# Ple product in the up projection's PSUM tiles, one norm chain for two pairs, weight tile and Gelu table loaded earlier

## The chip, the cores and the metric

The kernel runs on one core of a Trainium2 chip. The core has five engines, each with its own in-order stream of instructions: TensorE (PE, matmul), VectorE (DVE), ScalarE (ACT), GpSimd (POOL) and SyncE (SP, which mostly issues DMAs). Work passes between them through semaphores. The metric is the device time of one execution in microseconds, as the median of three runs. Every time below is in microseconds from the start of the profiled span, unless it says otherwise.

## The reference, cut to what matters

One layer of an encoder is applied to 1024 prompt frames and 32 sample frames, which the kernel handles together as 1056 columns.

```python
h = rms_norm(x, g_pre_mix)
z = h @ w_in                      # attention, HGRN2 and gate parts
ya = sink_attention(...)          # sliding window
yb = rms_norm(hgrn2(...)) * silu(ob)
mix = sigmoid(ga) * (ya @ w_br_a) + sigmoid(gb) * (yb @ w_br_b)
x = x + rms_norm(mix @ w_out, g_post_mix)          # output projection, x1
hf = rms_norm(x, g_pre_ffn)
a, u = split(hf @ w_up, 2)                         # up projection, 2 x 2816 columns
a = conv3(a)                                       # causal, depthwise
ffn = (gelu(a) * u) @ w_down
x = x + rms_norm(ffn, g_post_ffn)
x = x + (pe @ w_ple) * sigmoid(x @ w_ple_gate)     # "ple product" is pe @ w_ple
```

D_MODEL is 1024, D_FF 2816, and the width of pe 256. All is float32.

## The kernel before, in words

A float32 product is made of three matmuls in the form that TensorE reads quickly: both operands are split into a rounded part and a remainder, and high by high, low by high and high by low are added up in PSUM. These are the lines L200, L201 and L202 for an ordinary product (function `product`, through `block`, which takes a PSUM tile of one bank named `mm`) and L1835, L1836 and L1837 in the up projection (PSUM tiles named `st`).

The layer runs as a sequence of stages. The frames lie in four groups g of 264 columns (H = 264), which makes two pairs p, and the model dimension in eight tiles c of 128 rows. The stages around the change are:

- **Output projection.** For each pair p the loop runs over the eight row tiles c. Each step takes one weight tile of `w_out`, which was loaded by DMA as `wr` and split by ScalarE and VectorE into `wh` and `wl` (L181, L184), makes the two products of the pair and passes each to `z_out`, where ScalarE evicts it with a gain into `z` (L1449), squares it into `sq` (L1454), and VectorE adds the squares up (L1455). `next_w(n)` hands out a weight tile and keeps n tiles ahead loaded. During pair 1 the rest of the work of pair 0 is done beside it: `pair_norm(0, 0.25 / D)` turns sums of squares into the factors of the norm, `x1_part` adds the old x, `x1_squares` makes the squares of the new x, and a second call `pair_norm(0, 1.0 / D)` makes the factors of the next norm.
- **pair_norm.** TensorE multiplies the squares by a column of ones (`sums88`, L1475) into a PSUM bank named `tr`. VectorE works out the reciprocal roots in twelve small instructions on 128x6 elements. TensorE then transposes them (L301), and ScalarE copies the rows to `rbT` (L303).
- **Operand parts.** The up projection goes by a scheme with seven products of half-size blocks (Strassen's form), so its operands are sums and differences of blocks. `build_ops` makes them for the first pair of groups, and `op_part` for the second: ScalarE rounds (L1546), VectorE takes the remainder (L1547).
- **Ple product.** `ple_product(g)` makes, for each of the four groups, eight products of 128x264, in `mm` tiles; ScalarE copies each to `ple` (L1590), and a DMA on GpSimd's queue stores four at a time to `ple_d` (L1592). The table `beside`, filled through `at(m, f)`, names the work that is put behind the m-th of the 32 products: the adding of x for pair 1 (`x1_sum`, L1502, L1503), its gains (`x1_gain`, L1509), and the operand parts of the second pair.
- **Up projection.** Units of seven weight tiles each. Tiles 0 to 6 of unit 0 were split ahead, put to DRAM (`pw_d`), and come back by `load_part`; from unit 1 on, `unit_parts` makes them from raw weights `wu`: four sums of blocks (L1621, L1622, L1623, L1628, with the engine chosen as `adder`), a cast on ScalarE (L1614) and a remainder on VectorE (L1615). The results in PSUM are combined through `Sp` and `us` (L1846 to L1864). `ff_tail` is the end of a row tile: bias and first tap on ScalarE, two taps on VectorE (L1792), Gelu on ScalarE (L1794), gates on VectorE (L1795 to L1797).
- Unit 0 is special. It runs as two halves, one for each pair, and `last_ops` puts beside it what is left of the norm of pair 1.

The order within each engine comes from a scheduler that works from the code's order and from priorities (`behind(E)` puts a piece behind the work of an engine), and each engine then keeps this order: an instruction that waits holds back all that stand behind it on its engine. Pages of SBUF (`page(lq, i, ...)`) and buffers of pools are reused, and a transfer into one waits until its last reader has finished.

Of the kernel before, what the change touches and what calls it, by code (L numbers as in the profile page):

```python
# [59 lines left out]
def layer_kernel(  # L60
# [146 lines left out]
    def rsqrt(pool, out, v, n):  # L207

        bits = pool.tile([P, n], I32, tag="rsb", name=nm("rsb"), bufs=2)
        t = pool.tile([P, n], F32, tag="rst", name=nm("rst"), bufs=2)  # L210
# [1266 lines left out]
    def pair_norm(p, scale, t=None, late=False):  # L1477
# [3 lines left out]
        v = fo.tile([P, 6], F32, tag="nv", name=nm("nv"), bufs=2)  # L1481
        rs = fo.tile([P, 6], F32, tag="nr", name=nm("nr"), bufs=2)
# [4 lines left out]
        rsqrt(fo, rs[:], v[:], 6)  # L1487
# [18 lines left out]
    def x1_gain(g, i, ks=range(4)):  # L1506

        for k in ks:
            S.mul(z[g][:, 4 * i + k, :].bitcast(F32), x1q[g][i][:, k, :], g_ffn[:, 4 * i + k:4 * i + k + 1])  # L1509
# [24 lines left out]
    def x1_add(g):  # L1534

        a, b = x1q[g]
        V.tensor_tensor(a, a, b, op=ALU.add)
        V.tensor_tensor(a[:, 0:2, :], a[:, 0:2, :], a[:, 2:4, :], op=ALU.add)
# [43 lines left out]
    def ple_product(g, beside):  # L1582
        xs = pT.pop(g)
        for c in range(8):
            if c % 4 == 0:
                t = oz.tile([P, 4, H], F32, tag="x4", name=nm("ple"), bufs=3)
            b = block(ple_w[c // 4], slice((c % 4) * P, (c % 4 + 1) * P),
                      [xs[:, 0, k, :] for k in range(2)], [xs[:, 1, k, :] for k in range(2)],
                      ((0, 0), (1, 1)), H)
            S.copy(t[:, c % 4, :], b[:, :H])  # L1590
# [16 lines left out]
    def unit_parts(u, s1, place, out):  # L1607
# [10 lines left out]
        adder = V if u < 2 else G  # L1618
# [75 lines left out]
    for p in range(2):  # L1694
        for c in range(8):
            if p and c == 5:
                load_ple()
            w = next_w(2)
# [16 lines left out]
            if 2 <= c < 6:  # L1715
# [17 lines left out]

    for i in range(4):
        load_part(i)
    rows = pair_norm(1, 0.25 / D, late=True)
# [15 lines left out]
    at(6, rows, on=(E,))  # L1752
# [20 lines left out]
    qctx.close()  # L1773
    qctx = ExitStack()
    pf = qctx.enter_context(tc.tile_pool(name="pf", bufs=1, space=PSUM, reuse_waits="tile"))
# [24 lines left out]
    def last_ops(n):  # L1800
# [6 lines left out]
        with behind(S, V):  # L1807
# [306 lines left out]
```

## Time and profile before

| what | us |
| --- | --- |
| median of 3 runs | 2009.11 |
| the three runs | 2009.81, 2007.66, 2009.11 |
| the profiled execution | 2006.23 |
| its span | 2004.2 |
| pair 1 of the output projection | 1104 to 1158 |
| ple product | 1158 to 1185.3 |
| up projection, unit 0 | 1187.1 to 1211.5 |
| up projection, unit 1 | 1211.5 to 1233 |

The profiled execution is 2.03 us longer than its span, and 2.88 us shorter than the median. The stages follow from the lines that TensorE runs: L200 to L202 with `Ra`, `Rb` and `wh` in the output projection, with `pc` and `wq` in the ple product, and L1835 to L1837 in the up projection. A row such as "1150.34 0.63 PE L1475 ... [1.65 <-DVE sq L1528]" gives a start, a duration, the engine, the line, the operation and its tiles; the bracket says how long the engine had been idle and which instruction let it go on. A matmul of 264 columns is listed at 0.28 us, but the next one starts 0.12 us after it, since they overlap.

### The profile page before, as it was taken

What the parts mean: (1) busy time and instruction counts of PE and PEld (TensorE: products, weight loads), DVE (VectorE), ACT (ScalarE), POOL (GpSimd) and SP (SyncE); (2) the same over time, 40 slices, a digit from 0 to 9 for tenths busy, and PEclk for the clock granted to TensorE, in tenths of its full rate; (3) what the DMA queues carried; (4) which work ended last, traced back from release to release, by engine and by line L of the source; (5) the groups of instructions that cost most, each with busy time, mean ns of one, the idle gap of its engine ahead of it and who ended that gap; (6) DMA issues with size and microseconds to landing.
All of it is one profiled execution on the core that took longest, in us unless ns stands there. A gap on an engine that the chain in (4) does not pass through costs nothing. (4 is left out here: it accounts for less than half of the span.)

```text
span 2004.2 us, 37385 instructions
## 1 busy us (share of the span) xinstructions
PE 1981.8 (99%) x14304; PEld 1952.1 (97%) x14304; DVE 1423.3 (71%) x3150; ACT 967.7 (48%) x2178; POOL 224.8 (11%) x319
## 2 busy tenths in 40 slices
PE   8999999999999999999999999999999999999998
PEld 7899999999999999999999999999999999999998
DVE  6788888688888888553455778888878784655552
ACT  7555566556666666442224663333333344444432
POOL 1110100000000000002001123333333210000000
PEclk9999999999999999999999999999999999999999
DMA  7622311411111111477558582222222245655542
GB/s 257 154 92 85 107 52 55 152 43 58 58 39 53 37 54 54 136 235 220 164 173 278 182 278 66 84 75 86 76 86 76 86 140 195 212 191 173 170 130 80
DMA packets 253639, 247.47 MB, mean 123 GB/s; under 512 B 13893, under 2 KB 221912, under 8 KB 253461
## 3 DMA queue, kind: packets, MB, share of 16 engines
q1 hardware_dynamic: 245141, 218.59, 35.1%
q0 software_dynamic: 8240, 26.44, 3.8%
q8 instruction: 112, 1.84, 0.4%
q14 instruction: 66, 0.54, 0.1%
q10 hardware_dynamic: 80, 0.07, 0.0%
HBM read 177.56 MB, written 65.32 MB: 121 GB/s over the span
## 5 line engine op out<-in xcount | busy, mean ns | idle before, releaser
L1835 PE MATMUL st<-op,wt 128*128 128x264 f32 x1232 | 348.3, 283 | 3.5 <-ACT ple L1590 1.7
L1837 PE MATMUL st<-op,wt 128*128 128x264 f32 x1232 | 349.5, 284 | 0.0
L1836 PE MATMUL st<-op,wt 128*128 128x264 f32 x1232 | 347.7, 282 | 0.0
L184 DVE TENSOR_TENSOR wl<-wr,wh 128x1024 fp32r<-128x1024 f32 x129 | 157.9, 1224 | 118.9 <-ACT wh L181 105.5
L1835 PEld LDWEIGHTS st<-op,wt 128*128 128x128 f32 x1232 | 231.1, 188 | 4.6 <-ACT ple L1590 1.9
L1836 PEld LDWEIGHTS st<-op,wt 128*128 128x128 f32 x1232 | 231.4, 188 | 0.0
L1837 PEld LDWEIGHTS st<-op,wt 128*128 128x128 f32 x1232 | 230.8, 187 | 0.0
L181 ACT CAST wh<-wr 128x1024 fp32r<-128x1024 f32 x116 | 121.8, 1051 | 197.1 <-PE mm L201 149.7
L200 PE MATMUL mm<-La,wh 128*128 128x384 f32 (+1 forms) x528 | 174.4, 331 | 0.1
L200 PE MATMUL mm<-ac,wh 128*128 128x352 f32 x528 | 170.8, 324 | 1.3 <-DVE Sp L1864 1.3
L201 PE MATMUL mm<-Lb,wh 128*128 128x384 f32 (+1 forms) x528 | 170.9, 324 | 0.5 <-DVE Lb L710 0.4
L202 PE MATMUL mm<-La,wl 128*128 128x384 f32 (+1 forms) x528 | 170.5, 323 | 0.2 <-DVE wl L685 0.2
L201 PE MATMUL mm<-ac,wh 128*128 128x352 f32 x528 | 169.1, 320 | 0.0
L202 PE MATMUL mm<-ac,wl 128*128 128x352 f32 x528 | 169.1, 320 | 0.0
L1614 ACT CAST wt<-wu 128x512 fp32r<-128x512 f32 x126 | 77.7, 619 | 188.5 <-POOL ab L1821 93.8
L200 PE MATMUL mm<-Ra,wh 128*128 128x264 f32 x512 | 145.5, 284 | 0.0
L201 PE MATMUL mm<-Rb,wh 128*128 128x264 f32 x512 | 145.0, 283 | 0.0
L202 PE MATMUL mm<-Ra,wl 128*128 128x264 f32 x512 | 145.0, 283 | 0.0
L1615 DVE TENSOR_TENSOR wt<-wu,wt 128x512 fp32r<-128x512 f32 x126 | 101.0, 804 | 39.7 <-ACT wt L1614 39.7
L462 ACT ACTIVATE sc<-sc,st 128x257 f32<-128x257 f32 (+1 forms) x144 | 69.7, 485 | 73.2 <-DVE st L457 72.6
L201 PEld LDWEIGHTS mm<-Lb,wh 128*128 128x128 f32 x528 | 99.4, 188 | 1.7 <-DVE Lb L710 1.4
L200 PEld LDWEIGHTS mm<-ac,wh 128*128 128x128 f32 x528 | 99.0, 188 | 1.6 <-DVE Sp L1864 1.6
(496 smaller groups left out, 5692.8 us busy)
## 6 DMA issues: line engine op xcount, KB each, us to landing
wr<-in_w_down_dram SPq DMA_DIRECT2D x66, 512.0 KB
wu<-in_w_up_dram SPq DMA_DIRECT2D x42, 512.0 KB
wu<-in_w_in_dram SPq DMA_DIRECT2D x32, 512.0 KB
wr<-in_w_in_dram SPq DMA_DIRECT2D x25, 512.0 KB
ac<-act_d SPq DMA_DIRECT2D x66, 176.0 KB
act_d<-Up SPq DMA_DIRECT2D x21, 528.0 KB
wr<-in_w_out_dram SPq DMA_DIRECT2D x16, 512.0 KB
pw_d<-pw POOLq DMA_DIRECT2D x11, 512.0 KB, 5.3
```

The costliest lines, as they stand in the source:

```text
L181: S.copy(hi[:], raw[:])
L184: V.tensor_tensor(lo[:], raw[:], hi[:].bitcast(F32), op=ALU.subtract)
L200: E.matmul(ps, wh, a, start=first and n == 0, stop=False)
L201: E.matmul(ps, wh, b, start=False, stop=False)
L202: E.matmul(ps, wl, a, start=False, stop=last and n == len(ks) - 1)
L462: S.activation(sc[:m_, h, b0:e_ + 1], sc[:m_, h, b0:e_ + 1], AF.Exp, bias=st[:m_, 0, h:h + 1], scale=-1.0, accum_out=st[:m_, 1, h:h + 1])
L1614: S.copy(t[:, 0], src)
L1615: V.tensor_tensor(t[:, 1], src, t[:, 0].bitcast(F32), op=ALU.subtract)
L1835: E.matmul(o, wh, xh, start=first and k == 0, stop=False, skip_group_check=True)
L1836: E.matmul(o, wh, xl, start=False, stop=False, skip_group_check=True)
L1837: E.matmul(o, wl, xh, start=False, stop=k == 3, skip_group_check=True)
```

## The change

The ple product takes its PSUM from the pool `pf` of the up projection, which is now opened ahead of it. Two row tiles go to the two banks of one `st` tile, and one ScalarE copy of 128x528 takes the place of two of 128x264. The second norm of pair 0 and the first norm of pair 1 become one chain: their sums of squares go to one `tr` bank, one series of small VectorE instructions on twelve columns makes all factors, and `rows(1)` and `rows(0)` put the transposes behind the sixth and ninth ple products. Two of the operand parts of the first pair are written in the ple product's table, and the load of x for group 3 is put behind product 3 (page 0 instead of 1). One of four gains of groups 2 and 3 goes to VectorE. The last `w_out` tile is prepared one step earlier. The four sums of blocks of unit 1's weights go to GpSimd, as those of all later units did. In `last_ops`, `x1_add` is cut in two and spread over one more step, and a Gelu of one column is put there, whose result is overwritten later.

Line numbers after the change differ (L1601 is the copy that was L1590, L1865 to L1867 are the matmuls L1835 to L1837, L1632 is L1621).

```diff
@@ x_load, pair_norm, x1_gain, x1_add @@
-            t = page(lq, g - 2, [P, 8, H], "x")[:].bitcast(F32)
+            t = page(lq, 3 - g, [P, 8, H], "x")[:].bitcast(F32)
...
-            S.mul(z[g][:, 4 * i + k, :].bitcast(F32), x1q[g][i][:, k, :], g_ffn[:, 4 * i + k:4 * i + k + 1])
+            o, x, gain = z[g][:, 4 * i + k, :].bitcast(F32), x1q[g][i][:, k, :], g_ffn[:, 4 * i + k:4 * i + k + 1]
+            if g > 1 and k == 3:
+                V.tensor_scalar(o, x, gain, None, op0=ALU.mult)
+            else:
+                S.mul(o, x, gain)
...
         a, b = x1q[g]
         V.tensor_tensor(a, a, b, op=ALU.add)
+
+    def x1_fold(g):
+
+        a, b = x1q[g]
@@ ple_product @@
-            b = block(ple_w[c // 4], slice((c % 4) * P, (c % 4 + 1) * P),
-                      [xs[:, 0, k, :] for k in range(2)], [xs[:, 1, k, :] for k in range(2)],
-                      ((0, 0), (1, 1)), H)
-            S.copy(t[:, c % 4, :], b[:, :H])
+            if c % 2 == 0:
+                b = pf.tile([P, 2, 512], F32, tag="st", name=nm("st"), bufs=3)
+            product(b[:, c % 2, :H], ple_w[c // 4], slice((c % 4) * P, (c % 4 + 1) * P),
+                    [xs[:, 0, k, :] for k in range(2)], [xs[:, 1, k, :] for k in range(2)],
+                    ((0, 0), (1, 1)))
+            if c % 2:
+                S.copy(t[:, c % 4 - 1:c % 4 + 1, :], b[:, :, :H])
@@ unit_parts @@
-        adder = V if u < 2 else G
+        adder = V if u < 1 else G
@@ output projection @@
-            w = next_w(2)
+            w = next_w(2 + (p and c > 3))
...
-            if 2 <= c < 6:
+            if 2 <= c < 5:
                 next(op0)
...
             if c == 6:
-                for _ in op0:
-                    pass
                 x_load(2)
-                x_load(3)
-                with behind(E):
-                    rows = pair_norm(0, 1.0 / D, late=True)
                 p_load(2)
                 p_load(3)
-            if c == 7:
-                with behind(E):
-                    rows()
-
+
+    qctx.close()
+    qctx = ExitStack()
+    pf = qctx.enter_context(tc.tile_pool(name="pf", bufs=1, space=PSUM, reuse_waits="tile"))
     for i in range(4):
         load_part(i)
-    rows = pair_norm(1, 0.25 / D, late=True)
+    t = tr_bank()
+    v = fo.tile([P, 12], F32, tag="nv", name="nv2", bufs=1)
+    rs = fo.tile([P, 12], F32, tag="nr", name="nr2", bufs=1)
+    V.memset(v[:], 1.0)
+    for g in (0, 1):
+        sums88(t[:, 6:12], g, [sqz[g]])
+    for g in (2, 3):
+        sums88(t, g, [sqz[g]])
+    for a, sc in ((0, 0.25 / D), (6, 1.0 / D)):
+        V.tensor_scalar(v[:88, a:a + 6], t[:88, a:a + 6], sc, EPS, op0=ALU.mult, op1=ALU.add)
+    rsqrt(fo, rs[:], v[:], 12, 1)
+
+    def rows(p):
+        for h in range(2):
+            o, a = H * (2 * p + h), 6 * (1 - p) + 3 * h
+            norm_rows(rs[:, a:a + 3], T88, rbT[:, o:o + H])
...
-    at(6, rows, on=(E,))
+    for m in (0, 2):
+        at(m, next, op0)
+    at(3, x_load, 3)
+    at(6, rows, 1, on=(E,))
+    at(9, rows, 0, on=(E,))
@@ last_ops @@
-            elif n < 4:
-                x1_add(n)
-            elif n < 6:
-                op_part(1, n, (b11, b21)[n - 4])
+            elif n == 2:
+                x1_add(2)
+            elif n == 3:
+                x1_fold(2)
+                x1_add(3)
+                S.activation(us0[:, 0:1], ones[:], AF.Gelu_apprx_tanh)
+            else:
+                if n == 4:
+                    x1_fold(3)
+                if n < 6:
+                    op_part(1, n, (b11, b21)[n - 4])
```

The order on the engines shows three places. The first is TensorE at the start of unit 0, whose first half works through seven weight tiles, twelve matmuls each. `wt_14982` (before) and `wt_14933` (after) name the same tile, the fifth one, which comes from `pw_d` into a page that weights of the ple product (`wq`) held. Before, it is used behind the twelve matmuls each of four tiles, 48 in all, of which these rows show the end:

```order
L1837 MATMUL st_14961<-op_14336,wt_14595 128x264
L1835 MATMUL st_14962<-op_14423,wt_14982 128x264 [waits DMAHW0_49]
L1836 MATMUL st_14962<-op_14423,wt_14982 128x264
L1837 MATMUL st_14962<-op_14423,wt_14982 128x264
L1835 MATMUL st_14962<-op_14423,wt_14982 128x264
L1836 MATMUL st_14962<-op_14423,wt_14982 128x264
```

After the change, with 24 matmuls ahead of it:

```order
L1867 MATMUL st_14912<-op_14265,wt_14552 128x264
L1865 MATMUL st_14912<-op_14265,wt_14552 128x264
L1866 MATMUL st_14912<-op_14265,wt_14552 128x264
L1867 MATMUL st_14912<-op_14265,wt_14552 128x264
L1865 MATMUL st_14913<-op_14597,wt_14933 128x264 [waits DMAHW0_49,Activation_49]
L1865 MATMUL st_14911<-op_14338,wt_14554 128x264 [waits DMAHW5_49,Activation_49]
L1866 MATMUL st_14911<-op_14338,wt_14554 128x264
L1867 MATMUL st_14911<-op_14338,wt_14554 128x264
L1865 MATMUL st_14911<-op_14338,wt_14554 128x264
```

One matmul of that tile has moved ahead of the twelve of `wt_14554`, so that all of these stand behind its wait for a DMA.

The second place is ScalarE from the end of the ple product on. Before, the table that Gelu needs is loaded beside unit 1, between the casts of its weights (`wt`) and the Gelu of the first row tile (`a_15238`):

```order
L1846 COPY Sp_14959<-st_15251 128x528 [waits DVE_49,PE_49]
L1791 ACTIVATE a_15238<-ab_14963,cvec 128x1058 [waits DMASW4_49,DMASW6_49,DVE_49,Pool_49]
L1614 COPY wt_15394<-wu_15200 128x512 [waits PE_49,Pool_49]
L1794 ACT_TABLE_LOAD
L1794 ACTIVATE a_15238<-a_15238 128x1058 [waits DVE_49]
L1614 COPY wt_15422<-wu_15200 128x512 [waits PE_49]
```

After the change, in unit 0, behind the last copies of `ple`:

```order
L1601 COPY ple_14875<-st_14876 128x528 [waits DMASW3_49,PE_49]
L1554 COPY op_14838<-z_13365 128x1056 [waits DVE_49]
L1601 COPY ple_14875<-st_14890 128x528 [waits PE_49]
L1876 COPY Sp_14910<-st_14911 128x264 [waits DVE_49,PE_49]
L1536 ACTIVATE x_14481<-x_14481 128x1056 [waits DMASW5_49]
L1536 ACTIVATE x_14481<-x_14481 128x1056 [waits DMASW6_49]
L1536 ACTIVATE x_14625<-x_14625 128x1056 [waits DMASW0_49]
L1536 ACTIVATE x_14625<-x_14625 128x1056 [waits DMASW1_49]
L1839 ACT_TABLE_LOAD
L1839 ACTIVATE us_14909<-ones 128x1 [waits DMASW4_49]
L1554 COPY op_15003<-z_13364 128x1056 [waits DVE_49,Activation_49]
L1554 COPY op_15019<-z_13364 128x1056
```

The load of the table has moved ahead of the operand parts that are made beside unit 0, and stands with the squares of x (L1536).

The third place is GpSimd behind the last store of `ple`. Before:

```order
L1592 DMA ple_d<-ple_14916 128x4x264 [waits DMASW6_49,Activation_49]
L1821 MEMSET ab_14963 128x2 [waits DMASW5_49,DMASW6_49,DMASW3_49,DMASW2_49]
L1821 MEMSET ab_15254 128x2 [waits DMAHW1_49,PE_49]
L1621 TENSOR_TENSOR sa_15362<-wu_15202 128x512 [waits DMAHW0_49,DMAHW3_49,DVE_49,PE_49]
L1622 TENSOR_TENSOR wu_15202<-wu_15200,wu_15202 128x512 [waits DMAHW6_49,DMAHW4_49,DMAHW7_49,DMAHW2_49,Pool_49]
L1623 TENSOR_TENSOR wu_15200<-wu_15200,sa_15362 128x512 [waits DMAHW1_49,DMAHW5_49,DVE_49,Pool_49]
```

After the change:

```order
L1603 DMA ple_d<-ple_14875 128x4x264 [waits DMASW6_49,Activation_49]
L1851 MEMSET ab_14914 128x2 [waits DMASW5_49,DMASW6_49,DMASW3_49,DMASW2_49]
L1851 MEMSET ab_15206 128x2 [waits DMAHW1_49,PE_49]
L1632 TENSOR_TENSOR sa_15086<-wu_14931 128x512 [waits DMAHW2_49,DMAHW5_49,DMAHW1_49,PE_49]
L1633 TENSOR_TENSOR wu_14931<-wu_14929,wu_14931 128x512 [waits DMAHW4_49,DMAHW6_49,DMAHW3_49,DMAHW7_49,DMAHW0_49,Pool_49]
L1634 TENSOR_TENSOR wu_14929<-wu_14929,sa_15086 128x512 [waits DVE_49,Pool_49]
L1639 TENSOR_TENSOR wu_14929<-wu_14929 128x512 [waits DVE_49,Pool_49]
L1632 TENSOR_TENSOR sa_15314<-wu_15154 128x512 [waits DMAHW3_49,PE_49]
```

The four sums for unit 1 (`sa_15086`, and `wu_14931` and `wu_14929`) now stand on this engine, ahead of those of unit 2, which were the first there.

More of the change, by code (lines that the diff above doesn't have):

```diff
@@ L205, in layer_kernel, with rsqrt @@
     KS = tuple((k, k) for k in range(KT))
-    def rsqrt(pool, out, v, n):
-        bits = pool.tile([P, n], I32, tag="rsb", name=nm("rsb"), bufs=2)
-        t = pool.tile([P, n], F32, tag="rst", name=nm("rst"), bufs=2)
+    def rsqrt(pool, out, v, n, bufs=2):
+        bits = pool.tile([P, n], I32, tag="rsb", name=nm("rsb"), bufs=bufs)
+        t = pool.tile([P, n], F32, tag="rst", name=nm("rst"), bufs=bufs)
         V.tensor_scalar(bits[:], v.bitcast(I32), 1, None, op0=ALU.logical_shift_right)
@@ L1480, in pair_norm @@
         t = t or tr_bank()
[L1481 to L1482 removed]
+        v = fo.tile([P, 6], F32, tag="nv", name=nm("nv"), bufs=1)
+        rs = fo.tile([P, 6], F32, tag="nr", name=nm("nr"), bufs=1)
         V.memset(v[:], 1.0)
```

5 lines of the change are left out of this document (1 added, 4 removed).

## Prediction

> **What bounds the kernel now.** I read the page's first part, then the windows by stage, then TensorE's waits around the change, then its timeline at each wait and those of the engines that it waits for.
>
> ```profile
> span 2004.2 us, 37385 instructions
> PE 1981.8 (99%) x14304; PEld 1952.1 (97%) x14304; DVE 1423.3 (71%) x3150; ACT 967.7 (48%) x2178; POOL 224.8 (11%) x319
> 1104.00:1158.00 54.00, 52.14 (x441) 51.88 (x439) 42.35 (x76) 35.36 (x69) 6.78 (x9) 1.00 0.60 199
> 1158.00:1187.10 29.10, 27.02 (x218) 25.99 (x217) 21.70 (x30) 22.47 (x56) 8.28 (x11) 1.00 0.83 280
> 1187.10:1211.50 24.40, 23.60 (x192) 22.92 (x192) 19.20 (x42) 11.61 (x19) 0.94 (x3) 1.00 0.49 155
> 1211.50:1233.00 21.50, 20.46 (x167) 20.28 (x168) 17.88 (x28) 8.59 (x12) 8.92 (x5) 1.00 0.25 77
> ```
>
> The windows give length, then busy time and count of PE, PEld, DVE, ACT and POOL, granted clock, DMA share and GB/s. TensorE is busy 99 % of the span, and the change removes no matmul. It can win only the idle time of TensorE in the four stages that it touches, 129 us of 2004 (1104 to 1233): 54.00 − 52.14, 29.10 − 27.02, 24.40 − 23.60 and 21.50 − 20.46 make 5.8 us. The clock is 1.00 throughout, so no share of this is a slower clock. The list of TensorE's waits from 1055 to 1260 names most of it:
>
> ```profile
> PE st L1835 <- ACT ple L1590: 1.7, 1, 1.7
> PE tr L1475 <- DVE sq L1528: 1.7, 1, 1.7
> PE st L1835 <- DVE Sp L1853: 1.0, 1, 1.0
> PE st L1835 <- DVE us L1857: 0.5, 1, 0.5
> PE st L1835 <- DVE Sp L1864: 0.3, 1, 0.3
> ```
>
> These are 5.2 us. I cost each by the gap between neighbouring matmuls, whose undisturbed distance is 0.12 us, so that slow restarts count too.
>
> **The norm's sums.** TensorE stops once in the out projection, at the second half of pair 0's sums:
>
> ```profile
> 1150.34 0.63 PE L1475 MATMUL tr<-ones,sq 128*88 128x1 f32 x6 [1.65 <-DVE sq L1528]
> ```
>
> The change puts these sums behind the out projection's last products, at the end of that window (1158), some eight microseconds after the add that they wait for. The 1.65 us go. Late next may be the add of pair 1's last squares. Its sums stand at the same place before and after, and no wait for it is in the list of before, so I take −1.7; were it as late as the other one was, the wait would only have moved (0 to −1.7). The twelve small root instructions for one chain instead of two, and the last `w_out` tile a step earlier, move work on VectorE and ScalarE, where this window has 42.35 and 35.36 busy of 54.00: nothing for TensorE. The two operand parts written later, and the load of x for group 3, are covered by the ple stage, where VectorE has 7 us free (21.70 of 29.10).
>
> **Copies of ple.** In the last of its four groups TensorE outruns ScalarE:
>
> ```profile
> 1178.59 0.28 PE L202 MATMUL mm<-pc,wq 128*128 128x264 f32 x1
> 1178.84 0.39 PE L200 MATMUL mm<-pc,wq 128*128 128x264 f32 x1
> 1181.72 0.28 PE L202 MATMUL mm<-pc,wq 128*128 128x264 f32 x1
> 1182.27 0.39 PE L200 MATMUL mm<-pc,wq 128*128 128x264 f32 x1 [0.26 <-ACT ple L1590]
> L1590 ACT COPY ple<-mm 128x264 f32<-128x264 f32 x32 | 11.8, 400 | 5.8 <-PE mm L202 5.3 <-DMA ple_d<-ple 0.6
> L1509 ACT ACTIVATE z<-x,gvec 128x264 f32<-128x264 f32 x16 | 7.6, 536 | 0.0
> L1546 ACT CAST op<-z 128x1056 fp32r<-128x1056 f32 x5 | 5.6, 1117 | 0.0
> 1214.72 0.60 ACT L1846 COPY Sp<-st 128x528 f32<-128x528 f32 x1 [2.07 <-DVE ab L1790]
> ```
>
> Four such gaps, the first 0.25 and the last 0.55 between products, exceed 0.12 by some 1.1 us together, and the first matmul behind a gap is 0.39 long instead of 0.28, 0.1 more each: 1.5 us. The change makes 16 copies of 128x528 out of 32 of 400 ns; the nearest row for such a copy is 0.60 us, so ScalarE saves 12.8 − 9.6 = 3.2 us, and four gains of 536 ns leave it for VectorE, 2.1 us more, a quarter of the stage's 22.47. A cast of 1.12 us ahead of a copy still stands in TensorE's way here and there, so of the 1.5 I let 0.5 remain: −1.0 (0 to −1.5).
>
> **From ple to the up projection.** The switch shows as
>
> ```profile
> 1185.17 0.28 PE L202 MATMUL mm<-pc,wq 128*128 128x264 f32 x1
> 1187.12 0.39 PE L1835 MATMUL st<-op,wt 128*128 128x264 f32 x1 [1.66 <-ACT ple L1590]
> 1181.92 3.76 SPq L1672 DMA_DIRECT2D wt<-pw_d  x3
> DMA to landing us min/median/max: 3.4/5.9/8.6
> ```
>
> Before, the `st` pool is opened on the banks that the `mm` tiles give back, so the first `st` waits until ScalarE has emptied all `mm` tiles: 1.95 − 0.12 and the restart, 1.9 us. After, the first `st` tile of unit 0 takes a buffer emptied long ago, and the last copies run beside 24 matmuls of two blocks. This wait goes: −1.9.
>
> Something takes its place, though. The order shows that the first matmul with the fifth weight tile now stands 24 matmuls into unit 0, in place of 48. Its load goes into a page that ple's weights hold until 24 matmuls before the stage's end (that is when SP issues it, 1181.92). So TensorE needs the tile 24 + 24 matmuls after the issue: 48 x 0.12 = 5.8 us. Before, it had 24 + 48 matmuls and the 1.9 us besides, 10.5 us, and did not wait. The trace has no row for this load's landing; the nearest is the stores of ple, of about the same 512 KB at the same time, last row of the fence: median 5.9 us, longest 8.6, shortest 3.4. The wait lies between 0 and 8.6 − 5.8 = 2.8 us. The queues are at their fullest in this window (DMA share 0.83), so I take a landing halfway between median and longest, 7.2 us: +1.4.
>
> **Unit 0.**
>
> ```profile
> 1197.27 0.28 PE L1837 MATMUL st<-op,wt 128*128 128x264 f32 x1
> 1198.09 0.39 PE L1835 MATMUL st<-op,wt 128*128 128x264 f32 x1 [0.54 <-DVE us L1857]
> 1195.48 0.70 DVE L1538 TENSOR_TENSOR x<-x 128x528 f32<-128x528 f32 x1
> 1196.10 1.25 DVE L1547 TENSOR_TENSOR op<-z,op 128x1056 fp32r<-128x1056 f32 x1
> 1210.98 0.28 PE L1837 MATMUL st<-op,wt 128*128 128x264 f32 x1
> 1211.54 0.36 PE L1835 MATMUL st<-op,wt 128*128 128x264 f32 x1 [0.27 <-DVE Sp L1864]
> ```
>
> The first gap is 0.8 us with its restart too long: VectorE came to L1857 late because the sums of x1's squares (L1538, 0.70) and an operand's remainder (1.25) stood ahead of it. The change puts some of these sums a step later, the remainder stays: half goes, −0.4 (0 to −0.8). The second gap, 0.56 − 0.12 and a little restart, 0.5 us, follows VectorE's adds of weight blocks, four of 0.69 us, which go to GpSimd: −0.5 (0 to −0.5).
>
> **Gelu's table.**
>
> ```profile
> 1222.24 0.62 ACT L1614 CAST wt<-wu 128x512 fp32r<-128x512 f32 x1 [5.76 <-POOL ab L1821]
> 1222.88 1.28 ACT L1794 ACT_TABLE_LOAD   x1
> 1224.17 1.09 ACT L1794 ACTIVATE a<-a 128x1058 f32<-128x1058 f32 x1
> 1227.30 0.39 PE L1835 MATMUL st<-op,wt 128*128 128x264 f32 x1 [1.00 <-DVE Sp L1853]
> ```
>
> This is one chain: load, Gelu, VectorE's gate, then L1853, for which TensorE waits. TensorE's last matmul before it began at 1226.02, so the gap is 1.28, 1.16 too long and 0.1 restart. Without the load the chain is 1.28 earlier. The cast ahead of it still waits for GpSimd's sums of unit 2 (5.76 us idle), which does not improve, so I let 0.4 remain: −0.9 (−0.3 to −1.3). The load itself now lies in unit 0, where ScalarE works 11.61 of 24.40 us. The tiny Gelu behind it also waits for a store of ple, since it writes to memory that `ple` held. It is not the last of the stores, and ScalarE's four squares stand ahead of it, which should cover it; if not, the casts of the second pair's operands, which stand behind it, come late.
>
> **Adds on GpSimd.**
>
> ```profile
> 1195.42 0.19 POOL L1821 MEMSET ab<- 128x2 f32 x2 [7.03 <-DMA ple_d<-ple]
> 1204.14 0.69 DVE L1621 TENSOR_TENSOR sa<-wu 128x512 f32<-128x512 f32 x1
> L1621 POOL TENSOR_TENSOR sa<-wu x20: 1284/1288/2883, 1214.8 to 1602.6; 128x512 f32<-128x512 f32 x20
> L1622 POOL TENSOR_TENSOR wu<-wu,wu x20: 2183/2192/2224, 1217.7 to 1604.0; 128x512 f32<-128x512 f32 x20
> 1216.52 2.25 DVE L1792 SCALAR_TENSOR_TENSOR a<-ab,cvec,a 128x1058 f32<-128x1058 f32 x1
> 1237.49 1.32 DVE L1792 SCALAR_TENSOR_TENSOR a<-ab,cvec,a 128x1058 f32<-128x1058 f32 x1 [1.34 <-ACT a L1791]
> ```
>
> GpSimd is free from its memset at 1195.4 (0.19 long). It needs 1.29, 2.19 and 2.19 us for the first three sums (the third has the second's form), 5.7, where VectorE needs 0.69 each and ended the third about 1206.6. The cast of a sum stands in ScalarE's stream ahead of the copies to `rbT`, so a late sum holds back both. GpSimd starts when the raw weights have landed. If that is before 1206.6 − 5.7 = 1200.9, it costs nothing. The trace does not show that landing, only that it was over by 1204.14. I put +0.5 (0 to 1.5), as nearer to the free GpSimd at 1195.4 than to 1204.
>
> The sum: −1.7 − 1.0 − 1.9 + 1.4 − 0.4 − 0.5 − 0.9 + 0.5 = −4.5 us. The profiled execution took 2006.23 and would take 2001.7; against the median shown, 2009.11, which is 2.9 above it, the forecast is 2004.6 us.
>
> **The rivals.** *The weight tile lands late.* The landing takes 8.6 us as the slowest store did. Then the wait is 2.8, the sum −3.1, and the time 2006.0. For it speaks the DMA share; against it, that the median is 5.9.
>
> *All is hidden.* The tile lands within 5.8 us, the copies and the Gelu chain leave nothing, unit 0's first gap closes and GpSimd is early: −4.5 − 1.4 − 0.5 − 0.4 − 0.4 − 0.5 = −7.7, or 2001.4. Against it: several ends have to be met at once.
>
> *GpSimd and VectorE hold each other up, and unit 1 waits for its sums.* The L1621 of 2.88 us, against 1.29 in the median, ran while VectorE did L1792 in 2.25 instead of 1.32. The first three sums in unit 0 would take 1.29 + 2 x 2.19 = 5.7, and with 1.6 more for each 10.5. If GpSimd, held by late raw weights, starts only when VectorE does now, 1204.14, it ends at 1214.6 instead of 1206.6, 8.0 late. TensorE had no slack at 1211.54, so nearly all of this shows: −4.5 − 0.5 + 0.5 + 8.0 = +3.5, or 2012.6, slower than before. It costs something from a start past 1200.9 on, and it decides when the sums end some 4.5 us later than VectorE's did. Against it speaks that GpSimd is idle in unit 0 from 1195.4 on; for it VectorE's 19.20 busy of 24.40, which makes overlaps likely. [...]
>
> **How the numbers follow.** About 0.2 %, 4.0 us, is what a measurement can tell from no change here, so faster means below 2005.1. The forecast has a chance of 0.50; it stands so near that line that I split it 0.33 faster, 0.17 same. The late tile has 0.19, nearly all of it same (0.03 faster, 0.16 same). All hidden has 0.14, all faster. GpSimd has 0.17: 0.08 same, and 0.09 slower where VectorE is held up as well. Together: faster 0.50, same 0.41, slower 0.09. The range for 8 in 10 reaches from 2001.0, just under the best case, to 2010.0, short of the worst case at 2012.6; that leaves out most of the last rival and little else.
>
> **What would show it.** In the profile after: no wait of TensorE on L1528's add; none on a copy of ple at the first `st`, and instead one on a DMA 24 matmuls into unit 0, of 0 to 2.8 us (none: the landing was below 5.8); ple copies of 128x528 near 0.60 us; the table load among unit 0's squares, and the wait near 1226 shrunk to 0.4; GpSimd's first sums starting before 1201. The prediction is wrong if GpSimd's sums start well after that, if a DMA wait above 3 us stands in unit 0, or if new gaps come up in the out projection or in the units from the second on, whose order is unchanged.

## The result, and the profile after

| | before | after |
| --- | --- | --- |
| median, us (6 executions each, measured together) | 2008.38 | 2001.85 |
| lowest to highest | 2006.51 to 2012.32 | 2000.98 to 2002.58 |
| the profiled execution | 2006.23 | 2002.58 |
| its span | 2004.2 | 2000.8 |

The ratio is 0.9965, with a 95 % interval of 0.9952 to 0.9978. The changed kernel is faster by 6.5 us in the medians. The two profiled executions differ by 3.7 us only, and where the other 2.9 us are is the main question of what follows.

The first part of the page of the changed kernel, and its windows for the same four stages (out projection of pair 1, ple, units 0 and 1), moved to where these stages now lie:

```profile
span 2000.8 us, 37359 instructions
PE 1984.3 (99%) x14304; PEld 1955.0 (98%) x14304; DVE 1424.5 (71%) x3138; ACT 965.4 (48%) x2159; POOL 228.4 (11%) x323
1104.90:1157.00 52.10, 51.89 (x443) 51.71 (x441) 40.42 (x62) 35.02 (x68) 6.78 (x9) 1.00 0.58 192
1157.00:1183.25 26.25, 26.25 (x216) 25.84 (x215) 21.13 (x33) 18.08 (x34) 8.21 (x11) 1.00 0.85 291
1183.25:1208.57 25.32, 24.40 (x194) 23.06 (x193) 20.21 (x38) 14.65 (x23) 6.23 (x8) 1.00 0.56 176
1208.57:1230.20 21.63, 20.57 (x167) 20.36 (x168) 20.95 (x30) 7.81 (x11) 7.26 (x5) 1.00 0.27 87
```

The out projection and ple have lost nearly all of TensorE's idle time (1.86 and 2.08 us before, 0.2 and 0.0 now). Units 0 and 1 have not: 0.9 and 1.1 us are idle there, as before (0.8 and 1.0). In unit 1 VectorE is now busy 20.95 of 21.63 us. TensorE's list of waits from 1055 to 1260 shows which end is late there:

```profile
PE st L1865 <- DVE Sp L1878: 1.3, 2, 1.1
PE st L1865 <- ACT Sp L1876: 0.2, 1, 0.2
PE st L1865 <- DVE Sp L1883: 0.2, 1, 0.2
PE tr L301 <- DVE nv L1745: 0.2, 1, 0.2
PE st L1865 <- DVE us L1885: 0.2, 1, 0.2
```

The waits of 1.7, 1.7, 1.0 and 0.5 us of before are gone, and a new one of 1.1 us has come. The timeline of TensorE around the switch from ple to the up projection, at one of the short gaps of unit 0, and at the new wait:

```profile
1183.12 0.29 PE L202 MATMUL st<-pc,wq 128*128 128x264 f32 x1
1183.25 0.28 PE L1865 MATMUL st<-op,wt 128*128 128x264 f32 x1
...
1186.17 0.28 PE L1865 MATMUL st<-op,wt 128*128 128x264 f32 x1
1186.68 0.39 PE L1865 MATMUL st<-op,wt 128*128 128x264 f32 x1 [0.23 <-ACT Sp L1876]
...
1206.18 0.37 PE L1867 MATMUL st<-op,wt 128*128 128x264 f32 x1
1206.76 0.39 PE L1865 MATMUL st<-op,wt 128*128 128x264 f32 x1 [0.21 <-DVE Sp L1883]
...
1217.25 0.28 PE L1867 MATMUL st<-op,wt 128*128 128x264 f32 x1
1218.59 0.39 PE L1865 MATMUL st<-op,wt 128*128 128x264 f32 x1 [1.06 <-DVE Sp L1878]
```

The switch costs nothing now. The single matmul of the fifth weight tile (1186.17, 24 matmuls into unit 0) did not wait for its DMA. The matmul behind it waited a little for a copy. Of the two gaps that unit 0 had before (0.82 and 0.55 us from start to start, where 0.12 is undisturbed), the first is 0.45 now, at 1192. In place of the second there are three, of 0.48, 0.58 and 0.38, between 1203 and 1209.

All traces have 14304 matmuls, so the time of the k-th in one can be set against the k-th in the other. The difference, after less before, changes at the places below. It is not zero ahead of them (+0.8 us in the first pair of traces and +0.6 in the second, at 1147), from stages that the change does not touch; the table starts from there. The second pair are the two controls that are told of next.

| place (time in the trace of before) | forecast, us | first traces, us | controls, us |
| --- | --- | --- | --- |
| sums and norm chains (1147 to 1167) | −1.7 | −1.9 | −2.2 |
| copies of ple (to 1184) | −1.0 | −0.9 | −0.9 |
| switch, and unit 0 up to the copy to `Sp` (to 1191) | −0.5 (−1.9 + 1.4) | −1.4 (−1.9 + 0.5) | −1.4 |
| rest of unit 0 (to 1218) | −0.9 | +0.5 | +0.6 |
| unit 1 (to 1229) | −0.4 (−0.9 + 0.5) | +0.1 (−1.1 + 1.2) | +0.1 |
| start of the down projection (1640 to 1643) | 0 | −1.6 | −1.1 |
| first half of the down projection (to 1732) | 0 | +1.2 | +0.6 |
| all, to the last matmul | −4.5 | −4.0 | −4.4 |

### The profile page after: what moved, and what is told of

It reads as the page before. It is cut to its first block, busy times and chain, and to the rows that moved or that the text cites. A ratio compares the mean times of both kernels' runs of the same rounds, so it can differ in the third digit from the quotient of the medians.

```text
span 2000.8 us, 37359 instructions
## 1 busy us (share of the span) xinstructions
PE 1984.3 (99%) x14304; PEld 1955.0 (98%) x14304; DVE 1424.5 (71%) x3138; ACT 965.4 (48%) x2159; POOL 228.4 (11%) x323
## 4 chain that ended last, share of the span: by engine, by line
PE 92%; DVE 4%; ACT 2%; DMA 1%; issue 1%; POOL 0%; SPq 0%; DVEq 0%; ACTq 0%; POOLq 0%
PE mm L200 14%; PE mm L201 14%; PE mm L202 14%; PE st L1867 7%; PE st L1866 7%; PE st L1865 7%; PE G L1009 2%; PE Y L1006 2%; PE G L1008 2%; PE G L1006 2%; PE Y L1009 2%; PE Y L1008 2%; PE tr L478 1%; PE X L1006 1%; PE so L1200 1%; PE X L1009 1%
## 5 line engine op out<-in xcount | busy, mean ns | idle before, releaser
L1865 PE MATMUL st<-op,wt 128*128 128x264 f32 x1232 | 348.6, 283 | 2.0 <-DVE Sp L1878 1.3
L1867 PE MATMUL st<-op,wt 128*128 128x264 f32 x1232 | 349.8, 284 | 0.0
L1865 PEld LDWEIGHTS st<-op,wt 128*128 128x128 f32 x1232 | 231.2, 188 | 3.5 <-DVE Sp L1878 1.7
L1867 PEld LDWEIGHTS st<-op,wt 128*128 128x128 f32 x1232 | 230.9, 187 | 0.0
L202 PEld LDWEIGHTS mm<-La,wl 128*128 128x128 f32 x528 | 99.2, 188 | 0.7 <-DVE wl L685 0.5
```

The lines of the kernel that those rows point to most:

```text
L202: E.matmul(ps, wl, a, start=False, stop=last and n == len(ks) - 1)
L1865: E.matmul(o, wh, xh, start=first and k == 0, stop=False, skip_group_check=True)
L1867: E.matmul(o, wl, xh, start=False, stop=k == 3, skip_group_check=True)
```

## The experiments

**Controls.** Both kernels ran again, unchanged.

> The kernel before once more, unchanged. It shows what two profiles of one kernel differ by, and whether the 3.2 us between the two profiled spans (2004.2 and 2000.8 is 3.4) or the 6.5 us between the medians is the size of the change. Theory A (the profile has all of it, the rest is the spread of before's own runs): ratio 1.000 within 0.0015, and TensorE's times in the trace lie within 1 us of the first trace all along, with every gap between 1104 and 1230 the same to 0.1 us, and the wait of 1.3 us for VectorE at the start of the down projection there again. Theory B (before has a wait that comes and goes, and the first profile missed it): some gap of 2 us or more appears, or one of those known is gone.

Measured: 2009.88 us median, ratio 1.0004 (0.9995 to 1.0014). The trace repeats the first, with gaps of 2.14 us at the sums (1.87 in the first), 1.88 at the switch (1.94) and 1.16 at the down projection (1.61). So no gap of 2 us was missed in the first trace, which speaks against theory B as I had put it. Yet ten executions ran from 2005.46 to 2011.49, and the one with the profile is the fastest of them.

> The changed kernel once more. The kernel before had a spread of 6 us over 31 executions (2005.8 to 2011.7), the one with the joint norm chain had seven of ten executions within 1.4 us. Theory V (the wait at pair 0's sums differs between executions, since it hangs on the landing of x, and the joint chain takes it off the path): ten executions of the changed kernel lie within 3 us, median 2000.5 to 2003. Rival (the spread is the chip's, and six narrow executions were luck): a spread of 5 us and a median near 2004. The trace repeats the first one to 0.5 us, among it the pace of 0.1611 in the down projection, and no wait for the fifth weight tile at 24 matmuls.

Measured: 2002.11 us, ratio 0.9966 (0.9953 to 0.9979); five executions from 2001.23 to 2002.75. The spread belongs to the kernel before, not to the chip. The pace of the down projection did not repeat (below).

**Parts alone, in the kernel before.** First the two-bank tiles of the ple product:

```diff
+            if c % 2 == 0:
+                b = pf.tile([P, 2, 512], F32, tag="st", name=nm("st"), bufs=3)
+            product(b[:, c % 2, :H], ...)
+            if c % 2:
+                S.copy(t[:, c % 4 - 1:c % 4 + 1, :], b[:, :, :H])
```

> Before, with the two-bank tiles of the ple product alone (copies of 128x528, and the pool of the st tiles opened ahead of ple). Theory A (the parts add up): the gaps among ple's copies shrink from 1.5 to about 0.6 us and the switch to the up projection loses its 1.9, so TensorE is 2.8 us earlier at the start of unit 0, the other gaps stay. Theory R (rotation: 16 more st tiles shift the three buffers by one, which is what took away the wait of 1.3 us at the start of the down projection): that wait is gone here as well, 1.4 us more; together -4.2 in the trace up to that point. Rival to R (the wait is gone because VectorE runs otherwise after the Gelu table and the sums on GpSimd): the wait stays. As for the pace of the down projection's first half (0.1611 against 0.1589 us for one matmul): if it goes with the wait, 0.1611 here, else 0.1589.

Measured: 2008.04 us, ratio 0.9999 (0.9990 to 1.0009): no gain. Rows of TensorE's list of waits of this kernel:

```profile
PE tr L1475 <- DVE sq L1528: 1.7, 1, 1.7
PE st L1838 <- ACT Sp L1849: 0.8, 2, 0.4
PE st L200 <- ACT ple L1593: 0.8, 2, 0.4
PE st L1838 <- DVE us L1858: 0.8, 1, 0.8
PE st L1838 <- DVE Sp L1851: 0.8, 1, 0.8
```

The gap at the switch goes, and by 1191 TensorE has gained 1.2 us on the control (here and below, gains in a trace count from 1147, ahead of the change). But the copies of ple still hold TensorE up (0.8), and the units lose it again, 0.7 us in unit 1 and 1.7 in unit 2: TensorE comes early to work for which ScalarE and VectorE are as late as ever, or later. Theory A falls: the parts do not add up. The wait at the start of the down projection is gone here too, 1.1 us against the control and 1.6 against the first trace, as theory R had it. The first half of the down projection then loses 0.6 us of it: its matmuls follow each other every 0.1600 us, neither of the two values expected (more on this at the end).

What theory R means can be seen at the seventh matmul of the down projection, in the timeline of the kernel before, and then of the changed one:

```profile
1641.01 0.32 PE L202 MATMUL mm<-ac,wl 128*128 128x352 f32 x1
1642.62 0.43 PE L200 MATMUL mm<-ac,wh 128*128 128x352 f32 x1 [1.29 <-DVE Sp L1864]
```

```profile
1638.12 0.33 PE L202 MATMUL mm<-ac,wl 128*128 128x352 f32 x1
1638.29 0.32 PE L200 MATMUL mm<-ac,wh 128*128 128x352 f32 x1
```

The order of the matmuls is the same. But ple now takes 16 of the `st` tiles, which come from three buffers in turn, and 16 leaves a remainder of one. All later `st` tiles lie one buffer further on, the last one to be emptied lies in other banks, and the down projection's second `mm` tile no longer falls on it. In the order of the engines the wait for VectorE stands at the seventh matmul before, and at the nineteenth after.

Second, the joint norm chain alone, with nothing else changed:

```diff
-                with behind(E):
-                    rows = pair_norm(0, 1.0 / D, late=True)
...
+    for g in (0, 1):
+        sums88(t[:, 6:12], g, [sqz[g]])
+    for g in (2, 3):
+        sums88(t, g, [sqz[g]])
```

> Before, with the joint norm chain of twelve columns alone. Theory A: the wait of 1.65 us at the sums of pair 0 goes, nothing else moves by over 0.3 us: -1.7. Rival (the roots of both pairs now stand in ple's stage on VectorE, and the rows for pair 0 come late to the up projection, or the copies to rbT push ple's copies): the gaps in ple grow by 1 us or more, and the sum is -0.7 or less. The wait at the start of the down projection stays at 1.3 by theory R, since no st tile is added.

Measured: 2005.27 us, ratio 0.9990 (0.9981 to 1.0000). In the trace the wait for the squares is gone, and another has taken its place a few matmuls on:

```profile
PE mm L202 <- DVE wl L184: 1.3, 1, 1.3
```

It is the remainder of the last `w_out` tile, which VectorE makes behind the sums of squares that the wait had been for. The gap at the start of the down projection is still there (1.23 us), as theory R had it for a kernel without more `st` tiles. Third, the same with the tile prepared a step earlier:

```diff
-            w = next_w(2)
+            w = next_w(2 + (p and c > 3))
```

> Before, with the joint norm chain and the last w_out tile prepared a step earlier. The joint chain alone put a wait of 1.3 us for that tile's remainder (VectorE, L184) in the place of the wait for the squares. Theory A: with both the out projection has no gap over 0.5 us left, and TensorE is 1.6 us earlier at the start of ple than with neither; the gap at the switch to the up projection, 1.3 to 1.9 us, stays. Theory C (half clock): the spread of the kernel before comes from stretches at clock 0.50 that some executions have behind a gap of about 2 us; the gap at pair 0's sums, with matmuls of one column on both sides of it, is the main place. Then eight of ten executions lie within 2 us and have a mean clock of 0.999 or more, with a median near 2004.5. Rival (the gap of 1.9 us at the switch is as bad): the spread is 4 us or more, and clocks of 0.998 occur.

Measured: 2004.70 us, ratio 0.9975 (0.9965 to 0.9985). The out projection has no gap above 0.5 us left, and by 1167 TensorE has gained 2.1 us on the control; with the joint chain alone it was 0.5. So that term is the work of both parts. The eight executions run from 2002.77 to 2006.24, 3.5 us, wider than the 2 us that I had expected, but none has a clock below 0.999. The gap at the switch was 1.27 us here, so this does not tell what one of 1.9 would do. (This version, and below those with the gains on ScalarE, without the early table and run again for its time, ran on a second chip. The kernel before had medians of 2009.53 us there, and of 2008.18 and 2008.50 on the first.)

Fourth, the early table alone:

```diff
             elif n < 4:
                 x1_add(n)
+                if n == 3:
+                    S.activation(us0[:, 0:1], ones[:], AF.Gelu_apprx_tanh)
```

> Before, with the tiny Gelu in unit 0 alone (the table is loaded there). Theory A: the gap of 1.28 us near 1226 shrinks by 1.0 or more, and nothing comes in its place: -1.0. Rival (the gap of 1.34 us that the changed kernel has at 1217, a unit's fraction earlier, is the price of the earlier load, ScalarE being late with unit 1's casts): a new gap of about 1 us stands before it, and the sum is 0. By theory R the wait of 1.3 us at the start of the down projection stays.

Measured: 2008.10 us, ratio 1.0000 (0.9991 to 1.0010). In the trace the gap at 1226 shrinks by 0.6 us, a wait of 0.4 for the same instruction remains, and no gap comes in its place. The executions' spread of 5 us (2004.87 to 2010.32) hides 0.6.

**Parts undone, in the changed kernel.** The two norm chains apart again:

```diff
+                with behind(E):
+                    rows = pair_norm(0, 1.0 / D, late=True)
...
+    rows = pair_norm(1, 0.25 / D, late=True)
```

> The changed kernel with the two norm chains apart again, pair 0's at steps 6 and 7 of the out projection, everything else as changed. Theory V: the wait of 1.7 to 2 us at the second half of pair 0's sums is back in the trace, and the executions spread over 5 us again, with a median 3 to 5 us above the changed kernel's. Rival (the chain is worth its 1.7 us of the trace and no more): median +1.7 and no wider spread than the changed kernel's own.

Measured: 2005.32 us, 3.2 above the changed kernel's control, ten executions from 2003.23 to 2007.63. This trace caught what the others had not. Windows of this kernel (the columns as before; the third number from the end is the granted clock), then its timeline of TensorE:

```profile
1140.00:1149.00 9.00, 9.00 (x78) 9.00 (x77) 9.00 (x10) 7.47 (x14) 0.00 (x0) 1.00 0.92 338
1149.00:1151.30 2.30, 0.38 (x5) 0.30 (x4) 2.30 (x7) 1.49 (x4) 1.50 (x2) 0.98 0.72 194
1151.30:1155.00 3.70, 3.65 (x18) 3.65 (x19) 3.67 (x8) 0.76 (x3) 0.00 (x0) 0.50 1.03 395
1155.00:1158.00 3.00, 3.00 (x16) 3.00 (x15) 1.02 (x7) 0.08 (x1) 1.49 (x2) 0.50 0.65 189
1158.00:1160.00 2.00, 2.00 (x18) 2.00 (x18) 0.86 (x5) 0.68 (x2) 0.00 (x0) 0.99 1.03 387
```

```profile
1148.83 0.56 PE L1475 MATMUL tr<-ones,sq 128*88 128x1 f32 x6
1151.35 1.04 PE L1475 MATMUL tr<-ones,sq 128*88 128x1 f32 x6 [1.97 <-DVE sq L1532]
1152.62 0.42 PE L201 MATMUL mm<-Rb,wh 128*128 128x264 f32 x1
1152.84 0.42 PE L202 MATMUL mm<-Ra,wl 128*128 128x264 f32 x1
```

From the wait on the granted clock is 0.50, from 1151.2 to 1158.0. A matmul of 264 columns follows the last one after 0.22 us, not 0.12. The first 60 matmuls from the end of the wait on take 10.02 us here, and 7.02 in each of the four other profiles that have this wait: 3.0 us lost, besides the wait itself. The wait was 1.97 us, with matmuls of one column on both sides of it; waits of 1.65 to 1.92 us at the same place in the four other profiles left the clock at 1.00. Only this one of the five profiles shows it, and whether the wait's length or its moment decides is open.

That fits a part of the spread of the kernel before. Each execution has its mean granted clock on record, and sorted by it, all that ran beside the experiments (71) read:

| mean clock | executions | mean us | lowest to highest |
| --- | --- | --- | --- |
| 1.000 | 17 | 2006.6 | 2005.46 to 2008.07 |
| 0.999 | 22 | 2008.6 | 2006.42 to 2010.91 |
| 0.998 | 21 | 2009.9 | 2007.78 to 2012.30 |
| 0.997 | 11 | 2011.2 | 2009.89 to 2013.30 |

One such stretch takes 0.0017 off the mean clock (half of 6.8 us, in 2006), and the execution that has it reads 0.998. The mean also counts the end of the program: in all profiles the clock is 0.50 for the last 0.7 to 3.7 us, behind TensorE's last matmul, as in the control of the changed kernel, which reads 0.999:

```profile
1997.00:1999.50 2.50, 0.00 (x0) 0.00 (x0) 0.00 (x0) 0.00 (x0) 0.00 (x0) 0.50 0.30 87
```

A long end alone makes 0.999 out of 1.000 (half of 3.7 us, in 2006, is 0.0009). So 0.999 does not show a stretch of this length, and 0.997 can be one stretch with a long end as well as two. 32 of the 71 executions have 0.998 or less. At 3.0 us each that is 1.4 us in the mean, an estimate. It is not the whole spread: the executions of before with 0.999 lie 2.0 us above those with 1.000, and the kernel with the joint chain alone has two executions at 2008.13 and 2009.00 us, with 0.999, where the eight others end at 2006.99. What holds these up is open. So is a part of the 3.2 us above: only one of the ten executions here has 0.998, and the wait accounts for some 2 us in the others.

All eleven executions of the changed kernel have 0.999 or 1.000, and so have all of the two versions of the kernel before with the joint chain. The two kernels that keep the wait at the sums but not the one of 1.9 us at the switch (this one and the two-bank tiles alone) have 0.998 in 3 of 20 and never 0.997. Those with both waits (the 71, and the ten with the early table alone) have 0.998 or less in 37 of 81.

The gains of x1 all on ScalarE again:

```diff
-            if g > 1 and k == 3:
-                V.tensor_scalar(o, x, gain, None, op0=ALU.mult)
-            else:
-                S.mul(o, x, gain)
+            S.mul(o, x, gain)
```

> The changed kernel with all gains of x1 on ScalarE, as before. The two-bank tiles alone did not shorten the gaps among ple's copies. Theory A' (it is the four gains of 0.5 us taken off ScalarE that let the copies keep up): the gaps in the last group of ple are back, 1 us or more between 1176 and 1183, and TensorE comes 0.5 to 1.5 us later to unit 0. Rival (the chains' and parts' new places did it): no gap over 0.4 us, no difference.

Measured: 2002.16 us, no difference. The gaps in ple are back, as one of its rows shows:

```profile
PE st L200 <- ACT ple L1598: 0.8, 2, 0.4
```

TensorE comes 1.1 us later to the end of ple than in the control, and 0.8 of that remain to the end. So it is the gains, more than the larger copies, that closed the gaps; their worth is below what the medians can tell.

The table without its early load:

```diff
-                S.activation(us0[:, 0:1], ones[:], AF.Gelu_apprx_tanh)
```

> The changed kernel without the tiny Gelu; the table is loaded in unit 1 again. Alone in the kernel before it won 0.6 us in the trace, with a gap of 0.4 left. Theory A: a gap of 0.6 to 1.3 us comes up near 1224 and the median rises by 0.6 to 1.2. Rival (the gap of 1.34 us at 1217 that the contention of GpSimd and VectorE makes gives ScalarE time for the load): no new gap, no difference.

Measured: 2001.80 us. The rival holds in what it foresaw: there is no new gap, and the gap at 1217 is 1.34 us, unchanged. ScalarE loads the table behind it, 3.1 us earlier than before the change (1222.88), where TensorE is some 1.6 us earlier:

```profile
1219.77 1.28 ACT L1817 ACT_TABLE_LOAD   x1
```

In the changed kernel the early load is worth nothing. Whether TensorE's stop at 1217 makes the room for it, or that GpSimd begins unit 2's sums earlier (1211.8, before 1214.8), was not separated: no run lacks both the stop and the early load.

Unit 1's sums back on VectorE:

```diff
-        adder = V if u < 1 else G
+        adder = V if u < 2 else G
```

> The changed kernel with unit 1's four sums back on VectorE. Theory T1 (GpSimd's sums for unit 1 are late and are what made unit 0 lose 0.3 us four times and unit 1 1.34 us at 1217): those gaps shrink by 1 us or more together. Theory T2 (VectorE is the late one, and each sum on it costs 0.69 us): unit 0's gaps between 1203 and 1209 grow by 1 us or more, the gap at 1217 stays. My own account of the first trace leans to T2, as the sums were done on GpSimd by 1204.4 and two of them took 1.30 us where I had reckoned 2.19.

Measured: 2002.28 us, no difference. Unit 0 then has one gap at its end:

```profile
PE st L1865 <- DVE Sp L1894: 1.3, 1, 1.3
```

and the gap at 1217 is gone; by the end of unit 1 TensorE has gained 0.3 us on the control. Neither theory holds as it stood: the kernel's time is about the same with the sums on either engine (2002.28 against the control's 2002.11), and a stop at the one gap makes up for the other.

Unit 2's sums on VectorE:

```diff
-        adder = V if u < 1 else G
+        adder = V if u in (0, 2) else G
```

> The changed kernel with unit 2's four sums on VectorE as well as unit 0's, unit 1's on GpSimd. In the trace of the changed kernel GpSimd starts unit 2's sums at 1211.8, and VectorE's copy of two columns beside it takes 1.26 us, where others of its form take 0.16, and three remainders 2.98 where they took 1.89 before. Theory T3 (the two engines hold each other up there, and this makes the gap of 1.34 us at 1217): without GpSimd's sums in this place that copy takes 0.16, the remainders 1.9, and the gap goes, -1.2, less what four sums of 0.69 us on VectorE cost. Rival (VectorE is late from unit 0 on): the gap stays or grows by up to 2.8 us.

Measured: 2000.99 us, with four executions from 2000.39 to 2001.41. The gap at 1217 is gone, −1.3 us in the trace, and nothing is lost there for the four sums; the small gap at the copy to `Sp` in unit 0 was 0.5 us longer. The same stretch of VectorE and GpSimd in the changed kernel, and then VectorE's in this one:

```profile
1212.39 1.26 DVE L1810 COPY tails<-ab 128x2 f32<-128x2 f32 x1
1213.70 2.98 DVE L1626 TENSOR_TENSOR wt<-wu,wt 128x512 fp32r<-128x512 f32 x3
1211.81 1.82 POOL L1632 TENSOR_TENSOR sa<-wu 128x512 f32<-128x512 f32 x1 [4.02 <-PE st L1867]
1213.70 1.83 POOL L1633 TENSOR_TENSOR wu<-wu,wu 128x512 f32<-128x512 f32 x1
```

```profile
1212.01 0.15 DVE L1810 COPY tails<-ab 128x2 f32<-128x2 f32 x1
1212.22 1.88 DVE L1626 TENSOR_TENSOR wt<-wu,wt 128x512 fp32r<-128x512 f32 x3
```

A copy of two columns takes 1.26 us beside GpSimd and 0.15 alone, and three remainders 2.98 and 1.88. Theory T3 holds. It was run again for its time:

> The version with unit 2's sums on VectorE once more, for its time: median 2001.0 within 0.5 us, 1.0 below the changed kernel, ratio to the kernel before 0.996 with an interval of 0.0015 to either side; the gap of 1.34 us at 1217 is gone again, and no execution has a clock below 0.999.

Measured: 2000.77 us, ratio 0.9957 (0.9945 to 0.9970); five executions from 2000.42 to 2002.15, none with a clock below 0.999. Nine executions together have a median of 2000.8, the changed kernel's eleven 2002.0. This is the fastest version here.

## Why the prediction was right, and where it was not

The forecast was 2004.6 us and faster, within 2001.0 to 2010.0. The time came out at 2001.85, in the range and on the right side, and the sum agrees with the traces (−4.5 against −4.0 and −4.4) better than its terms do. That is luck: against the first traces the stretches of the table are off by −0.9, +1.4, +0.5, −1.6 and +1.2 us, besides smaller ones, and these cancel. The time itself was forecast 2.7 us too high, because the sum was taken from a median that lay 2.9 us above the profiled execution, and most of those 2.9 us went as well. Of the signs that the prediction named, the waits for L1528 and at the first `st` are gone, and GpSimd began before 1201. But no wait for a DMA came, and a new gap of 1.34 us stands in unit 1, which comes near to what it had called a sign of being wrong.

- *The norm's sums.* −1.9 and −2.2 against −1.7. But the term was put down to the move of the sums alone, and the earlier `w_out` tile was costed at nothing. Alone the move wins 0.5 us, as the tile's remainder is late next; the two together win it all. And in one profiled execution, with the two chains apart, 3.0 us went besides the wait of 1.97 us, at a clock of 0.50: no row of the trace of before showed this.
- *Copies of ple.* −1.0 was −0.9. The two reasons given for it were not equal: the four gains matter, the wider copies alone did not shorten the gaps (two of 0.67 and 0.69 us in place of four of 0.25 to 0.54).
- *The switch.* −1.9, as forecast. The weight tile in its place, +1.4, was 0. The tile's loads were issued from here on:

```profile
1180.39 3.25 SPq L1683 DMA_DIRECT2D wt<-pw_d  x3
```

  and the matmul that needs the tile ran at 1186.17 without a wait, so it landed within 5.8 us. In none of the profiles of the changed kernel and its variants did TensorE wait for a DMA in unit 0. I had taken 7.2 from the stores; the median of these, 5.9, was nearer.
- *Unit 0.* This is the step that failed: −0.4 and −0.5 were forecast, and +0.5 came, besides another 0.5 in its first matmuls, most of it for the copy to `Sp`. The first gap shrank as forecast, from 0.82 to 0.45. The second did not go with the sums that left VectorE: three gaps stand in its place, and those with a wait in the list end with VectorE's work on `Sp`. The whole unit takes 25.3 us, 0.9 more than before (with the sums back on VectorE it takes 25.6). TensorE arrives 4 us earlier, and what VectorE and ScalarE have to finish for it does not. The one-sided bounds (0 to −0.8 and 0 to −0.5) left this out.
- *Gelu's table.* −0.9 was forecast and −1.1 measured at its place. Yet the run without it shows that the kernel does not gain from it: the load then falls at 1219.77, and no gap comes of it.
- *GpSimd's sums.* They started at 1198.6, before 1200.9, and did not hold up unit 1. What I had described as the rival, the two engines holding each other up, came with the sums of unit 2, which were on GpSimd before too; since TensorE's progress starts them, they now fall on VectorE's work for unit 1. The price was 1.2 us, not 8.
- *Not in the sum at all.* The rotation of the `st` buffers (−1.1 to −1.6), the down projection's pace (+0.6 to +1.2, which comes with the same two-bank tiles), and the clock. The prediction said that the units from the second on keep their order. On TensorE they do, but the same order with other buffers does not have the same waits. Against the 17 executions of before with a clock of 1.000 (2006.6) the changed kernel's 2002.0 is 4.6 us faster, and the mean of all 71 (2008.9) is 2.3 us above that. Of these 2.3 us the clock has 1.4 by the estimate above, and the rest is open. A clock of 0.50 from the wait at the sums on is shown by one trace of five. That the wait of 1.9 us at the switch brings it too is only likely, from 37 in 81 executions against 3 in 20, and which share each has stays open.

## What to carry to other kernels

A gap of TensorE can be dearer than it looks in one profile: with a gap of 1.97 us another 3.0 us went, at a clock of 0.50, in one execution that was caught, so look at the spread and the mean clock of all executions before believing one trace. An engine made earlier at one stage wins only what its suppliers can follow, so cost an edit with the next late engine named, and try it alone and undone: the two-bank tiles here won nothing alone, and the early table nothing in the changed kernel. When a pool is shared between stages, count the tiles modulo its buffers.

## What the runs showed that I had not expected

The clock of 0.50 behind a gap of 1.97 us is told above. Two more things are new.

Matmuls of 352 columns at the start of the down projection run at a steady pace that differs between profiles: 0.1589 us each in the two of before, 0.1611 and 0.1600 in the two of the changed kernel, all at a granted clock of 1.00. The windows of the first profile of each show it (159 matmuls against 157 in 25 us):

```profile
1665.00:1690.00 25.00, 25.00 (x159) 25.00 (x159) 11.01 (x11) 10.49 (x15) 0.00 (x0) 1.00 0.47 154
```

```profile
1661.00:1686.00 25.00, 25.00 (x157) 25.00 (x157) 11.37 (x12) 11.31 (x16) 0.00 (x0) 1.00 0.51 169
```

It is worth 0.6 to 1.2 us. The other traces show what it goes with: it is 0.1589 in the three other kernels without two-bank tiles in ple (the joint chain, with and without the earlier tile, and the early table), and 0.1600 in the kernel before with these tiles alone and in all six profiles of the variants of the changed kernel. So the tiles that move the wait away also cost 0.6 us of pace. Why they do, and why one profile has 0.1611, was not tried.

GpSimd's sum of two 128x512 blocks, which took 2.19 us in all units before, took 1.30 in unit 1 of the changed kernel:

```profile
1200.00 1.30 POOL L1633 TENSOR_TENSOR wu<-wu,wu 128x512 f32<-128x512 f32 x1
```

VectorE ran mostly small instructions of six columns beside it and the sum ahead of it, and two of these (at 1198.79 and 1200.18) took 1.15 us where the others took 0.17. So 2.19 is not the least that the sum takes on GpSimd. That the other 0.89 us come from VectorE's work beside it is my reading of these rows; no run tried it alone.
